# Two transformer blocks on one core: the pace and place of the row fetches beside the router

## The chip, the cores and the metric

One core of a Trainium2 chip runs the whole program. The metric is the device time of one execution in microseconds; the figure of the kernel before is the median of three runs, 1791.49 us (1789.15 to 1792.43). Matrix products run on TensorE (PE, with its weight loads in a row of their own, PEld), elementwise work on VectorE (DVE) and ScalarE (ACT). SyncE (SP) issues the streamed weight loads, GpSimd (POOL) issues the gathers. All DMAs run on the same 16 DMA engines.

## The reference, cut to what matters

Two blocks follow one another on 256 tokens of width 1024, in f32. Each block is a mixer (projections, attention or retention or recurrence, an output projection) and then a PEER layer; the change is in the PEER layers alone:

```
q = (xb @ w_q)                    # 8 heads, 2 halves of 128
s1, s2 = q1 @ k1.T, q2 @ k2.T     # 128 keys a half
top 16 of each half, then the top 16 of their 256 sums -> 16 experts a head, gates g = softmax
h = sum_d u[idx] * x              # u: 16384 x 1024
y = sum_k gelu(h) * g * v[idx]    # v: 16384 x 1024
```

So each token picks 128 of 16384 experts (8 heads of 16), and needs their rows of `u` and of `v`.

## The kernel before, in words

**Two ways to the experts.** `G` = 104 tokens have their rows gathered from HBM, one gather per 128 (token, head, expert) places: 104 row fetches from `u`, then 104 from `v`, each 128 rows of 1024 f32 into one tile `rows`. The other `N` = 152 tokens go through all 16384 experts densely: 128 products with blocks of `u` (`products_of`, L1434), a gate matrix from one-hots (`gate_product`, L1394) and 128 products with blocks of `v` (L1491).

**Stages of one PEER layer, all in the program order of PE.** (1) The queries: 32 units, 16 per tile of 128 tokens (`for t`, `for hc`); each is 8 accumulated products with a 512 KB block of `w_q` (L1322), and the score products of two units earlier (L1311). (2) 128 units of `u`. (3) 128 units of `v`. The weights of all three come as a stream of 512 KB loads (`load_to`, L98) from SP into 4 + 3 buffers; a load goes out as soon as a buffer is used up.

**The router** (`routing`, a generator) runs on DVE beside stages 1 and 2. For tile 0 it takes the heads in order: `route_head` picks the 16 best of either half and of the sums (`best16`, L1194 to L1202), and after every second head `decode` (L1226 to L1249) turns places into expert numbers `eif` (L1272). Then `spread` copies these to the places of the gathers: 12 small products on PE (L1147) that read `eif`, and copies on ACT into `ei` (L1156). From then on `fetch_rows` may issue the gathers of these heads from POOL (L1089). After tile 0 come the eight heads of tile 1, two larger decodes, the softmax, and transposes on PE (L1296). Only when the generator is at its end (`not side`) do the 38 gate blocks (`at`) begin, spread over the remaining units of `u`.

**Who paces what.** After each unit `beside(us, rows)` adds `rows` to a goal and uses gathered rows up to it (`use_rows`; on DVE L1103 for `u`, L1112 for `v`), each use letting `fetch_rows` issue one more gather. Then it lets the router go on by `step(1000.0 * us - 1310.0 * rows, 1)`: the budget is in planned nanoseconds of DVE, and each piece of the router yields its planned cost. In the queries `rows` is 0 for tile 0 and 0.3 a unit for tile 1; in stage 2 it is 0.5 a unit before the first gate block and 0.98 from there; in stage 3 the rest is spread evenly (`pace`). A row has 5 buffers of its own and 3 that are free while whole blocks stream, so up to 8 can be fetched or waiting. The heads known so far bound it too (`fetch["known"]`).

**Scales by column.** `scales_by_column` (L1184, 4 products on PE) and `scaled` (L1190, 4 multiplications on DVE) make `un`, the normalised activations of the dense tokens, which the first unit of stage 2 reads. They stand beside units 8 to 12 of tile 1.

**Order.** Every engine runs its instructions in the order in which the program above emits them; semaphores between engines are put in by the framework.

Of the kernel before, what the change touches and what calls it, by code (L numbers as in the profile page):

```python
# [51 lines left out]
def two_blocks_kernel(ctx: ExitStack, tc: tile.TileContext, a: dict, out: bass.AP, dbg=None, stop=None):  # L52
# [156 lines left out]
    def bank_b(name):  # L209
        return pp_b.tile([P, 512], F32, tag="b", name=name)  # L210
# [788 lines left out]
    def peer(which, norm, names, shared, gelu, after):  # L999
        keys_name, gain_name, u_rows, v_rows = names  # L1000
        with ExitStack() as es:
# [67 lines left out]

            order = [list(col), sorted(col)]  # L1070
            fetch = {"known": 0, "issue": 0, "use": 0, "goal": 0.0}
            fetched, acc, folds = {}, {}, []
            in_rows = [0, 0]

            def fetch_rows():
                while fetch["issue"] < 2 * G:
                    n = fetch["issue"]
                    c, j = divmod(n, G)
                    key = order[c][j]
                    if key[1] >= fetch["known"]:  # L1080
                        return
                    if in_rows[0] < ROW_BUFS[0]:
                        k, t = 0, gp.tile([P, D], F32, tag="rows", name="rows")
                    elif in_rows[1] < ROW_BUFS[1] and n < 2 * G - 8 and units[st["use"] - 1][0] in WHOLE:
                        k, t = 1, spl_p.tile([P, D], F32, tag="lo", name="rows")
                    else:
                        return
                    in_rows[k] += 1
                    nc.gpsimd.indirect_dma_start(  # L1089
                        out=t, out_offset=None, in_=tables[c],  # L1090
                        in_offset=bass.IndirectOffsetOnAxis(ap=ei[:, col[key]:col[key] + 1], axis=0))
                    fetched[n] = k, t, clock[0]
                    fetch["issue"] += 1
# [98 lines left out]
            def best16(v, i, s, w, cost):  # L1192
# [9 lines left out]
                nc.vector.max_index(i[:, 8:16], v[:, 8:16], w)  # L1202
                yield cost

            def route_head(t, h):

                for c in range(2):
                    yield from best16(v_t[:, c, :], i_t[:, h, t, c, :], s_all[:, h, t, c, :], tmp, 320)
                v1, v2 = v_t[:, 0, :], v_t[:, 1, :]
                for o, a0, na, nb in ((0, 0, 1, 16), (16, 1, 3, 8), (40, 4, 4, 4), (56, 8, 8, 1)):  # L1210
                    sh = [P, na, nb]
                    nc.vector.tensor_tensor(
                        cand[:, o:o + na * nb].rearrange("p (a b) -> p a b", a=na),
                        bc(v1[:, a0:a0 + na, None], sh), bc(v2[:, None, 0:nb], sh), op=ALU.add)
                yield 660
                yield from best16(top[:, t, h, :], pos[:, t, h, :], cand, tmp[:, 0:64], 270)
# [46 lines left out]
            def routing():  # L1263

                for h in range(8):
                    while not heads[0]:
                        yield None
                    yield from route_head(0, heads[0].pop(0))
                    if h % 2:
                        yield from decode(0, h - 1, 2)  # L1270
                        hs = slice(h - 1, h + 1)
                        nc.vector.scalar_tensor_tensor(  # L1272
                            eif, fid[:, 0, 0, hs, :].rearrange("p h k -> p (h k)"), 128.0,
                            fid[:, 1, 0, hs, :].rearrange("p h k -> p (h k)"), op0=ALU.mult, op1=ALU.add)
                        w = G // 4
                        spread(eif, 2, ei[:, (h // 2) * w:(h // 2 + 1) * w])
                        fetch["known"] = h + 1
                        fetch_rows()
                exps(0)
                for h in range(8):  # L1280
                    while not heads[1]:
                        yield None
                    yield from route_head(1, heads[1].pop(0))
                    if h == 0:
                        softmax(0)
                        spread(gt[:, 0].rearrange("p h k -> p (h k)"), 8, gg)
                    if h == 3:
                        yield from decode(1, 0, 4)
                exps(1)
                yield from decode(1, 4, 4)  # L1290
                softmax(1)
                pts = [tpp.tile([P, 512], F32, tag="tp", name="pt") for c in range(2)] + [bank_b("pt")]
                for c, pt in enumerate(pts):
                    for t in range(2):
                        v = gt[:, t] if c == 2 else fid[:, c, t]
                        nc.tensor.transpose(pt[:, t * P:(t + 1) * P], v.rearrange("p h k -> p (h k)"), ident)  # L1296
                yield None
                for c, pt in enumerate(pts):
                    nc.scalar.activation(idx[:, c, :], pt[:, G:T], AF.Copy)
                yield None  # L1300
                yield None
# [26 lines left out]
            def beside(us, rows=0.0):  # L1328

                clock[0] += us  # L1330
                fetch["goal"] += rows
                use_rows(int(fetch["goal"]))
                step(1000.0 * us - 1310.0 * rows, 1)

            for t in range(2):
                for hc in range(16):
                    q = query(t, hc)
                    if t == 0 and hc == 0:
                        square_sums(x_ss, 0, (1,))
                        scales(0)  # L1340
                    nc.scalar.activation(qts[hc % 4], q, AF.Copy)
                    if t == 0 and hc == 1:
                        scales_done(0)
                        to_plain(1, range(4, 8), norm)
                        nc.vector.scalar_tensor_tensor(gain, x_sb[:, 0, :], rs[:, 0:1], gain, op0=ALU.mult, op1=ALU.mult)
                        side.append(routing())
                    if hc > 1:
                        score(t, hc - 2)
                    elif t == 1:
                        score(0, hc + 14)  # L1350
                    if t == 0 and hc == 2:
                        square_sums(x_ss, 1, (1,))
                        scales(1)
                    if t == 0 and hc == 3:
                        scales_done(1)
                    if t == 0 and hc == 4:
                        for g in range(ng):
                            own_rows(g)
                    if t == 1 and hc == 8:
                        by_column = scales_by_column()  # L1360
                    if t == 1 and 9 <= hc < 13:
                        scaled(by_column, 2 * (hc - 9))
                    beside(2.05, 0.3 * t)

            sh = [P, 4, P]
            io = bc(iota[:, None, :], sh)
# [71 lines left out]
            for n in range(NE):  # L1438
# [21 lines left out]
                if n >= 2:  # L1460
                    hidden_apply(n - 2)
                hidden(n)
                beside(2.45 if at else 2.07, 0.98 if at else 0.5)
            assert len(at) == NB and at[-1] + 4 < NE
            hidden_apply(NE - 2)
            hidden_apply(NE - 1)
# [263 lines left out]
```

## Time and profile before

| | |
|---|---|
| median of three runs | 1791.49 us |
| the profiled execution's own time | 1787.17 us |
| its span | 1785.1 us |
| PE busy | 1730.7 us, 97% |
| PE weight loads busy | 1617.5 us, 91% |
| DVE / ACT / POOL busy | 64% / 33% / 29% |
| moved by DMA | 590.69 MB, mean 331 GB/s |
| mean granted TensorE clock | 0.994 |
| chain that ended last | PE 75%, DMA 18%, DVE 3%, issue 2% |

The span runs from the first to the last instruction on the chip; 2.07 us of the profiled execution lie around it. Layer 1's PEER part fills about 257 to 931 us of the span, layer 2's about 1094 to 1773 us. A line of the chain of waits names what the last instruction hung on, step by step backwards; a share there is time on that path, while a busy share is not.

### The profile page before, as it was taken

What the parts mean: (1) busy time and instruction counts of PE and PEld (TensorE: products, weight loads), DVE (VectorE), ACT (ScalarE), POOL (GpSimd) and SP (SyncE); (2) the same over time, 40 slices, a digit from 0 to 9 for tenths busy, and PEclk for the clock granted to TensorE, in tenths of its full rate; (3) what the DMA queues carried; (4) which work ended last, traced back from release to release, by engine and by line L of the source; (5) the groups of instructions that cost most, each with busy time, mean ns of one, the idle gap of its engine ahead of it and who ended that gap; (6) DMA issues with size and microseconds to landing.
All of it is one profiled execution on the core that took longest, in us unless ns stands there. A gap on an engine that the chain in (4) does not pass through costs nothing.

```text
span 1785.1 us, 32628 instructions
## 1 busy us (share of the span) xinstructions
PE 1730.7 (97%) x12468; PEld 1617.5 (91%) x12468; DVE 1135.8 (64%) x2694; ACT 597.4 (33%) x1643; POOL 509.5 (29%) x456
## 2 busy tenths in 40 slices
PE   8999998999999999999999998999999999999997
PEld 6878888999999999989988777899999999989997
DVE  5555658797678864444455545789767885444444
ACT  6665542322666520000007564231266660000001
POOL 0000012122344444444411001212234445444440
PEclk9999999999999999999999999999999999999999
DMA  7433569899999999999985226989999999999995
GB/s 267 145 116 132 177 195 343 299 364 393 389 402 418 411 413 419 419 418 419 419 321 197 96 74 217 354 299 380 377 396 416 417 404 419 418 419 419 418 419 218
DMA packets 162219, 590.69 MB, mean 331 GB/s; under 512 B 18272, under 2 KB 18432, under 8 KB 161808
## 3 DMA queue, kind: packets, MB, share of 16 engines
q1 hardware_dynamic: 99648, 362.07, 53.3%
q0 software_dynamic: 62128, 226.22, 32.1%
q8 instruction: 98, 1.61, 0.3%
q14 instruction: 57, 0.47, 0.1%
q10 hardware_dynamic: 288, 0.33, 0.1%
HBM read 585.40 MB, written 1.05 MB: 329 GB/s over the span
## 4 chain that ended last, share of the span: by engine, by line
PE 75%; DMA 18%; DVE 3%; issue 2%; ACT 1%; SPq 0%; ACTq 0%; DVEq 0%
PE h L1434 30%; DMA raw<-in_v_dram 16%; PE y L1491 15%; PE pj L296 5%; PE pj L298 5%; PE q L1322 5%; PE pj L297 5%; PE g L1394 4%; DMA raw<-in_w_q_dram 1%; PE spread L1147 1%; PE sc L476 1%; PE hs L797 1%; PE sps L1311 1%; DMA x_sb<-in_x_dram 0%; PE o L296 0%
## 5 line engine op out<-in xcount | busy, mean ns | idle before, releaser
L1491 PE MATMUL y<-XA,raw 128*128 128x152 f32 x4096 | 556.9, 295 | 14.5 <-DMA raw<-in_v_dram 8.7
L1491 PEld LDWEIGHTS y<-XA,raw 128*128 128x128 f32 x4096 | 534.2, 190 | 39.7 <-DMA raw<-in_v_dram 33.5
L1434 PE MATMUL h<-un,raw 128*128 128x152 f32 x4096 | 544.0, 293 | 0.0
L1434 PEld LDWEIGHTS h<-un,raw 128*128 128x128 f32 x4096 | 533.0, 190 | 0.0
L1089 POOL DMA_INDIRECT rows<-in_u_rows_dram,ei x208 | 223.8, 1076 | 489.1 <-DVE hg L1103 271.5
L1089 POOL DMA_INDIRECT rows<-in_v_rows_dram,ei x208 | 263.6, 1268 | 318.2 <-DVE acc L1112 248.5
L1112 DVE SCALAR_TENSOR_TENSOR acc<-rows,ag,acc 128x1024 f32<-128x1024 f32 x202 | 259.5, 1285 | 2.8
L1103 DVE CUSTOM_DVE_ANT_0 rows<-rows,xg 128x1024 f32<-128x1024 f32 x208 | 253.0, 1218 | 0.0
L116 ACT ACTIVATE hi<-raw 128x1024 fp32r<-128x1024 f32 (+1 forms) x109 | 114.3, 1052 | 339.3 <-DMA raw<-in_w_in_dram 288.4
L1502 DVE MEMSET XA<- 128x1 f32 x128 | 7.6, 59 | 285.7 <-PE y L1491 238.5
L117 DVE TENSOR_TENSOR lo<-raw,hi 128x1024 fp32r<-128x1024 f32 (+1 forms) x109 | 132.5, 1221 | 84.4 <-ACT hi L116 83.7
L1322 PE MATMUL q<-act,raw 128*128 128x128 f32 x1024 | 132.2, 283 | 11.1 <-issue 7.6
L1322 PEld LDWEIGHTS q<-act,raw 128*128 128x128 f32 x1024 | 125.0, 198 | 14.6 <-issue 9.2
L296 PE MATMUL pj<-hi,act 128*128 128x512 f32 x320 | 131.6, 411 | 2.2 <-ACT hi L116 1.3
L298 PE MATMUL pj<-hi,act_l 128*128 128x512 f32 x320 | 125.7, 393 | 0.1
L297 PE MATMUL pj<-lo,act 128*128 128x512 f32 x320 | 125.7, 393 | 0.0
L1422 ACT ACTIVATE XA<-h 128x152 f32<-128x152 f32 (+36 forms) x252 | 65.9, 262 | 159.6 <-PE h L1434 153.0
L1036 POOL DMA_DIRECT2D gain<-in_gain_dram x2 | 1.1, 534 | 398.8 <-PE out L298 252.9
L1520 ACT ACTIVATE XA<-y 128x384 f32<-128x384 f32 (+1 forms) x6 | 2.5, 456 | 290.9 <-DVE XA L1519 290.9
L1399 DVE TENSOR_TENSOR XA<-g,XA 128x216 f32<-128x216 f32 (+18 forms) x76 | 40.6, 535 | 83.5 <-PE g L1394 33.1
L1394 PE MATMUL g<-b,b 128*128 128x128 f32 x608 | 80.1, 275 | 0.0
L1419 ACT ACTIVATE hb<-h 128x4 f32<-128x4 f32 (+36 forms) x148 | 36.8, 249 | 121.1 <-PE h L1434 110.9
(371 smaller groups left out, 1823.3 us busy)
## 6 DMA issues: line engine op xcount, KB each, us to landing
raw<-in_u_dram SPq DMA_DIRECT2D x256, 512.0 KB
raw<-in_v_dram SPq DMA_DIRECT2D x256, 512.0 KB
raw<-in_w_in_dram SPq DMA_DIRECT2D x79, 512.0 KB
raw<-in_w_q_dram SPq DMA_DIRECT2D x64, 512.0 KB
raw<-in_w_out_dram SPq DMA_DIRECT2D x16, 512.0 KB
raw<-in_w_mix_dram SPq DMA_DIRECT2D x12, 512.0 KB
rows<-in_u_rows_dram,ei POOLq DMA_INDIRECT x208
rows<-in_v_rows_dram,ei POOLq DMA_INDIRECT x208
```

Source lines behind the costliest of these rows:

```text
L116: nc.scalar.activation(hi[:, c], src[:, c], AF.Copy)
L117: nc.vector.tensor_tensor(lo[:, c], src[:, c], hi[:, c].bitcast(F32), op=ALU.subtract)
L296: nc.tensor.matmul(ps[t], lhsT=ah, rhs=wh[:, j, :], start=(k == 0), stop=False)
L297: nc.tensor.matmul(ps[t], lhsT=ah, rhs=wl[:, j, :], start=False, stop=False)
L298: nc.tensor.matmul(ps[t], lhsT=al, rhs=wh[:, j, :], start=False, stop=(k == last))
L1089: nc.gpsimd.indirect_dma_start(out=t, out_offset=None, in_=tables[c], in_offset=bass.IndirectOffsetOnAxis(ap=ei[:, col[key]:col[key] + 1], ...
L1103: nc.vector.tensor_tensor_reduce(t, t, xg[:, g, :], 1.0, 0.0, ALU.mult, ALU.add, hg[:, k:k + 1])
L1112: nc.vector.scalar_tensor_tensor(acc[g], t, ag[:, k:k + 1], acc[g], op0=ALU.mult, op1=ALU.add)
L1322: nc.tensor.matmul(q, lhsT=w[:, k * P:(k + 1) * P], rhs=acts["x"][:, k, t * P:(t + 1) * P], start=(k == 0), stop=(k == KT - 1))
L1394: nc.tensor.matmul(gs[k][:, j, :], lhsT=b2[:, j, :], rhs=b1[:, j, :], start=True, stop=True)
L1434: nc.tensor.matmul(hs[n], lhsT=w[:, k * P:(k + 1) * P], rhs=un[:, k, :], start=(k == 0), stop=(k == KT - 1))
L1491: nc.tensor.matmul(block(d), lhsT=w[:, d * P:(d + 1) * P], rhs=XA[:, n, :], start=(n == 0 and d % nb == 0), stop=(n == NE - 1), skip_group ...
```

## The change

Five edits, all in `peer`, so all of them count twice. While the current unit is one of `w_q`, a gather is issued only if fewer than 4 are issued and not yet used. The spread of the expert numbers, with the `known` and `fetch_rows` behind it, and the spread of tile 0's gates, are put off until the next head has emitted the first of its two column searches. The scales by column move from tile 1's units 8 to 12 to tile 0's units 7 to 11. The rates go from 0.3 to 0.4 rows a unit in tile 1's queries and from 0.5 to 0.62 in stage 2 before the first gate block; the planned budget of the router goes from 1000 to 1050 a microsecond. And the generator gives way once more between the last softmax and the transposes.

```diff
-                    if key[1] >= fetch["known"]:
+                    if key[1] >= fetch["known"] or units[st["use"] - 1][0][0] == "w" and n - fetch["use"] >= 4:
                         return
...
+            def known(h):
+                w = G // 4
+                spread(eif, 2, ei[:, (h // 2) * w:(h // 2 + 1) * w])
+                fetch["known"] = h + 1
+                fetch_rows()
...
                 for c in range(2):
+                    while c and pending:
+                        pending.pop(0)()
                     yield from best16(v_t[:, c, :], i_t[:, h, t, c, :], s_all[:, h, t, c, :], tmp, 320)
...
-                        w = G // 4
-                        spread(eif, 2, ei[:, (h // 2) * w:(h // 2 + 1) * w])
-                        fetch["known"] = h + 1
-                        fetch_rows()
+                        pending.append(lambda h=h: known(h))
...
-                        spread(gt[:, 0].rearrange("p h k -> p (h k)"), 8, gg)
+                        pending.append(lambda: spread(gt[:, 0].rearrange("p h k -> p (h k)"), 8, gg))
...
                 softmax(1)
+                yield None
...
-                step(1000.0 * us - 1310.0 * rows, 1)
+                step(1050.0 * us - 1310.0 * rows, 1)
...
-                    if t == 1 and hc == 8:
+                    if t == 0 and hc == 7:
                         by_column = scales_by_column()
-                    if t == 1 and 9 <= hc < 13:
-                        scaled(by_column, 2 * (hc - 9))
-                    beside(2.05, 0.3 * t)
+                    if t == 0 and 8 <= hc < 12:
+                        scaled(by_column, 2 * (hc - 8))
+                    beside(2.05, 0.4 * t)
...
-                beside(2.45 if at else 2.07, 0.98 if at else 0.5)
+                beside(2.45 if at else 2.07, 0.98 if at else 0.62)
```

## Rows read from the trace of the kernel before

**Rows 1.** Windows: length; busy us of PE, PEld, DVE, ACT, POOL; clock, DMA share, GB/s.

```profile
291.50:303.42 11.92, 8.03 (x40) 7.53 (x39) 8.70 (x35) 1.27 (x5) 3.74 (x4) 0.71 1.02 411
303.42:340.90 37.48, 35.75 (x319) 35.56 (x319) 28.52 (x129) 10.85 (x45) 4.06 (x5) 1.00 0.83 277
340.90:443.00 102.10, 102.10 (x796) 102.10 (x796) 92.56 (x349) 25.31 (x77) 27.25 (x26) 1.00 0.98 372
443.00:643.00 200.00, 200.00 (x1593) 200.00 (x1592) 151.08 (x318) 117.25 (x422) 81.36 (x74) 1.00 1.01 405
643.00:931.00 288.00, 281.40 (x2049) 267.19 (x2048) 137.15 (x173) 2.64 (x3) 124.30 (x97) 1.00 1.01 407
...
700.00:720.00 20.00, 19.35 (x142) 18.23 (x141) 8.26 (x12) 0.00 (x0) 8.19 (x7) 1.00 1.03 419
...
1131.44:1142.72 11.28, 7.55 (x40) 6.94 (x39) 8.52 (x33) 1.31 (x5) 3.74 (x4) 0.71 1.02 403
...
1482.60:1773.30 290.70, 282.76 (x2063) 268.97 (x2062) 138.73 (x177) 2.32 (x4) 124.12 (x98) 1.00 0.99 401
```

**Rows 2.** Timeline of PE around 300 us: start, duration, what, idle before.

```profile
291.72 0.97 PE L1322 MATMUL q<-act,raw 128*128 128x128 f32 x5
...
297.20 0.59 PE L1322 MATMUL q<-act,raw 128*128 128x128 f32 x2 [1.72 <-issue]
...
299.58 3.62 PE L1322 MATMUL q<-act,raw 128*128 128x128 f32 x16
...
303.42 1.96 PE L1322 MATMUL q<-act,raw 128*128 128x128 f32 x16
...
305.44 1.95 PE L1322 MATMUL q<-act,raw 128*128 128x128 f32 x16
```

**Rows 3.** Timeline of POOL over the first gathers of layer 1.

```profile
286.43 1.00 POOL L1089 DMA_INDIRECT rows<-in_u_rows_dram,ei  x1 [19.63 <-ACT ei L1156]
...
295.22 0.93 POOL L1089 DMA_INDIRECT rows<-in_u_rows_dram,ei  x1 [0.30 <-issue]
305.38 0.94 POOL L1089 DMA_INDIRECT rows<-in_u_rows_dram,ei  x1 [9.22 <-DVE XA L1200]
```

**Rows 4.** Timeline of DVE in the same stretch.

```profile
295.08 0.18 DVE L1226 TENSOR_SCALAR XA<-XA 128x32 uint32<-128x32 uint32 x1 [0.84 <-DVE XA L1202]
```

**Rows 5.** The page's costliest groups: busy, mean ns, idle before.

```profile
L1491 PEld LDWEIGHTS y<-XA,raw 128*128 128x128 f32 x4096 | 534.2, 190 | 39.7 <-DMA raw<-in_v_dram 33.5
L1434 PE MATMUL h<-un,raw 128*128 128x152 f32 x4096 | 544.0, 293 | 0.0
...
L1103 DVE CUSTOM_DVE_ANT_0 rows<-rows,xg 128x1024 f32<-128x1024 f32 x208 | 253.0, 1218 | 0.0
```

**Rows 6.** Chain of waits, layer 1: the first 17 units of stage 3.

```profile
643.14 35.15 PE y L1491 x272
```

**Rows 7.** Timeline of PE: spreads of layer 1 in the queries, transposes in stage 2.

```profile
284.25 1.51 PE L1147 MATMUL spread<-eif,c_sel 128*128 128x32 f32 x12
...
331.23 1.51 PE L1147 MATMUL spread<-eif,c_sel 128*128 128x32 f32 x12 [1.73 <-DVE eif L1272]
...
443.04 0.60 PE L1296 MATMUL pt<-ident,XA 128*128 128x128 f32 x4
```

**Rows 8.** Timeline of DVE: second head, its decode, expert numbers; next decode's end; softmax.

```profile
272.49 0.29 DVE L1194 MAX8 XA<-XA 128x8 f32<-128x128 f32 x1 [1.17 <-ACT XA L1314]
...
277.46 0.18 DVE L1226 TENSOR_SCALAR XA<-XA 128x32 uint32<-128x32 uint32 x1
...
284.00 0.19 DVE L1272 SCALAR_TENSOR_TENSOR eif<-XA 128x32 f32<-128x32 f32 x1
...
302.92 0.19 DVE L1272 SCALAR_TENSOR_TENSOR eif<-XA 128x32 f32<-128x32 f32 x1
...
435.04 0.29 DVE L1261 TENSOR_TENSOR gt<-gt,XA 128x128 f32<-128x128 f32 x1
```

**Rows 9.** DVE groups of layer 1's queries: the multiplications that make `un`.

```profile
L1190 DVE TENSOR_TENSOR un<-act,rows 128x304 f32<-128x304 f32 x4 | 1.9, 464 | 7.4 <-PE rows L1184 7.4
```

More of the change, by code (lines that the diff above doesn't have):

```diff
@@ L1071, in peer @@
             fetch = {"known": 0, "issue": 0, "use": 0, "goal": 0.0}
-            fetched, acc, folds = {}, {}, []
+            fetched, acc, folds, pending = {}, {}, [], []
             in_rows = [0, 0]
```

## The prediction

> **What bounds the kernel now.** The windows by stage come first, because each stage has its own limit [rows 1]. In stage 2 PE is busy for the whole of both windows (102.10 of 102.10 us, 200.00 of 200.00 us), and the page's group of its products has no idle time before it [rows 5]: PE is the bound there, with DMA at 372 and then 405 GB/s. In stage 3 the link runs at 407 GB/s over 288 us, its tail included (419 inside it), and PE's weight loads stand idle for 39.7 us in the two layers, 33.5 of them ended by a landing block of `v` [rows 5]: there the link is the bound. The chain shows what PE alone would need: the first 17 units, whose blocks had landed ahead, took 35.15 us, 2.068 us a unit [rows 6], so 128 take 264.7 us. Layer 1 used 288.0, layer 2 290.7 [rows 1]. The first ends with the next mixer's loads, the second with its folds; either way some 20 us a layer are lost to bytes.
>
> The queries are odd. PE takes 2.02 us a unit where nothing stops it (303.42 to 305.44) [rows 2]. The two units from 291.50 to 303.42 took 11.92 us [rows 1]. [...] DVE has holes in the same microseconds (0.84 us before L1226) [rows 4]. Just before, from 286.43, POOL issued eight gathers back to back, the eighth at 295.22 [rows 3]. The same stands in layer 2, 11.28 us for two units [rows 1]. I read it as one event: a burst of gathers that holds up every engine, whatever carries it.
>
> **The limit of four.** The stall's price is 11.92 - 2 x 2.02 = 7.88 us and 11.28 - 4.04 = 7.24 us. PE broke off as the fifth of the eight gathers was being issued (one each 1.26 us from 286.43) [rows 2, 3]. With the limit, four go out at the first `known`, and the next only as one is used. Blocks of `w_q` had to share the link with the burst, but PE didn't wait for them, so they lose no cover. I take the stall as gone: -15.1 us in both layers. The bounds: nothing gained, and the whole of it. What is late next: at the first use in stage 2 the limit falls away, three are left and five go out back to back, just where the stall set in. The nearest row is the old burst, in which PE had no gap until the fifth; I take 1 us a layer, between 0 and another 7.9. Net -13.1 us.
>
> [...]
>
> **The rates.** The planner's numbers can be added by hand. Before: 16 x 0.3 + 51 x 0.5 + 77 x 0.98 = 105.8, so 105 rows are used when stage 3 begins. That the first gate block stands at unit 51 follows from the trace too: the transposes at 443.04 [rows 7] come after unit 47 (443.04 - 340.9 us, less two spreads of 1.25 and two score products of 0.2, are 48 units of 2.068), and the generator gives way three more times behind them. After: the router's share of a unit in stage 2 is 1050 x 2.07 - 1310 x 0.62 = 1361 planned ns, where it was 1000 x 2.07 - 1310 x 0.5 = 1415. Some 48 units at 1415 are 67.9 us of plan; less about 1.4 that the wider budgets in the queries do earlier, 66.5 / 1361 is 49 units. With the extra pause the first block comes at 53. Then 16 x 0.4 + 53 x 0.62 + 75 x 0.98 = 112.8: 112 rows, seven more.
>
> A row fetch moves 128 x 1024 f32, 0.524 MB, as a unit does. At the 419 GB/s that stage 3 carries while PE waits for it [rows 1] it takes 1.251 us. Before, stage 3 uses 103 rows beside 128 blocks: 231 x 1.251 / 128 is 2.26 us a unit against PE's 2.068; after, with 96 rows, 2.19 us. The link stays the bound, so seven fetches are worth 7 x 1.251 = 8.76 us a layer, -17.5 us. The bounds: nothing, if PE begins to wait in stage 2 instead, and 8.76. For that I weigh the load there: 1.62 x 0.524 / 2.068 is 411 GB/s before the first gate block, where 372 passed in the trace, and from the first block on it stays near the 405 of before [rows 1]. Both lie under 419, the first by 2%, and it begins with the five fetches at once. I take the full gain less 1 us a layer for waits of PE: -15.5 us.
>
> **Spreads and scales.** In the queries PE waited 1.73 us for `eif` at the third spread and hardly at the first [rows 7]; layer 2 shows the same pair. The wait at the third goes: its spread comes a unit later. The first gets worse. The four multiplications cost DVE 464 ns each [rows 9], and three now lie ahead of the first `eif`; DVE was already the one that PE met there (284.00 + 0.19 against 284.25) [rows 7, 8]. Since the first column search fits into the same unit's budget, the spread isn't put off past a product: +1.4 us. Queued behind that waiting spread on PE are the next unit's products, and behind `ei` the gathers.
>
> Then DVE has no stall to catch up in. A head takes it 277.46 - 272.49 = 4.97 us for 5.21 planned, a decode with its `eif` 284.19 - 277.46 = 6.73 for 5.0 [rows 8]: two heads and a decode are 16.7 for 15.4. From the first to the second `eif` it needs some 17 us (302.92 - 284.00, less 2.5 for five holes, the longest of which stands in [rows 4], plus the fourth multiplication), PE about 17.3: no wait. For the third, 16.7 and five rows at 1.22 us [rows 5] are 22.8, PE's ten units and a spread 21.5, 1.3 us short with 0.3 of margin left from the second; the fourth is alike, with a little less. I take 1.2 us for these together, with 0 and 3 as bounds. 1.4 + 1.2 - 1.73 is +0.85 us a layer, +1.7. The transposes hold: DVE's softmax was done at 435.33, PE came at 443.04 [rows 7, 8], 7.7 us, and PE comes 4 us later now. `scales_by_column` itself is four products of PE, moved and not added. On ACT and SP nothing moves but the copies behind the spreads.
>
> **The sum.** -13.1 - 15.5 + 1.7 = -26.9 us. The profiled execution took 1787.17 us (span 1785.1), so 1760.3; the median of the timed runs lies 4.3 above the profiled one, so I predict 1764.6 us.
>
> **The rivals.**
> 1. *The stall stays, or comes in stage 2 instead.* For it: five gathers still go out together there, and PE broke off at the fifth. Against it: three fewer follow. Then only the rows' gain is left: 1791.5 - 15.5 + 1.7 = 1777.7 us.
> 2. *The link takes the gain back.* Stage 2 at 411 GB/s finds the link full, PE waits there for `u`, and stage 3 begins with less landed. For it: 411 is all that the stall's window moved, with work queued throughout. Against it: 405 passed for 200 us with PE never waiting. Then the stall's gain is left: 1791.5 - 13.1 + 1.7 = 1780.1 us.
> 3. *Slower: any burst of four or more stalls.* Then there are two a layer, at the first `known` and at the start of stage 2, each with its stretch at the lower clock. The old stall's 7.6 us and the 7.76 - 0.85 = 6.9 that rows and spreads leave make 14.5, so it turns slower once a burst costs more than 7.25 us. At 12, the eight-gather stall and half again, it is 24 - 14.5 = 9.5 us a layer, 1810.5 us. Against it: PE ran through the first four without a gap [rows 2, 3].
> 4. *Only recorded executions stall.* Then timed runs have nothing of it to lose, and again 1777.7 us. For it: the holes of PE and DVE come together and have no semaphore. [...]
> 5. *It does little:* the bursts never form or the rows land as before, 1791 us.
>
> **How the numbers follow.** Forecast 0.60 (own range 1754 to 1773), rival 1 0.14, rival 2 0.11, rival 3 0.06, rival 4 0.05, rival 5 0.04. A measurement here can tell about 0.2%, 3.6 us, from no change. Faster: the forecast and rivals 1, 2 and 4, 0.60 + 0.14 + 0.11 + 0.05 = 0.90, less 0.04 for cases that meet: 0.86. Slower: rival 3 and a piece of these, 0.07. Same: 0.07. The range takes in rivals 1, 2 and 4, both bounds of the burst and of the link, and leaves out rivals 3 and 5 and the tails: 1753 to 1782 us.
>
> **What would show it.** Right: no gap inside a query unit and a clock of 1.00 in both layers; at most four gathers back to back there; queries of about 76 us, where 257.64 to 340.90 are 83.3 now; 96 gathers used in stage 3 and 8 to 9 us less in each. Wrong: a stretch of "issue" gaps at the first units of `u`, idle time before L1434, or stage 3 as long as now. The first spread should wait 1 to 2 us for `eif`, the third not at all.

## The result, and the profile after

The changed kernel took 1758.96 us (median of 4 runs, 1755.73 to 1760.83), the kernel before 1790.88 beside it (4 runs, 1789.15 to 1792.43): a ratio of 0.982, 95% interval 0.980 to 0.984. The forecast was 1764.6. The profiled execution took 1755.73 us with a span of 1754.0, 31.1 us under that of before, where the sum said 26.9.

The windows of the changed kernel, stage 2 ahead of the transposes, stage 2 from there, stage 3 of layer 1 and 20 us within it (length; busy us of PE, PEld, DVE, ACT, POOL; clock, DMA share, GB/s), answer to [rows 1]:

```profile
332.40:441.00 108.60, 108.60 (x848) 108.60 (x847) 100.16 (x364) 26.34 (x80) 37.45 (x36) 1.00 1.02 413
441.00:635.00 194.00, 194.00 (x1545) 194.00 (x1544) 148.91 (x305) 116.32 (x418) 81.94 (x72) 1.00 1.02 407
635.00:918.00 283.00, 277.60 (x2059) 267.81 (x2057) 130.96 (x169) 3.57 (x4) 112.85 (x91) 1.00 1.00 404
700.00:720.00 20.00, 20.00 (x156) 19.92 (x155) 9.95 (x13) 0.00 (x0) 7.95 (x7) 1.00 1.03 419
```

PE is still busy for the whole of stage 2, though 413 GB/s pass where 372 did. Stage 3 is 7 us shorter in layer 1. The page's groups (answer to [rows 5]) say by what: idle time ahead of `v`'s weight loads is 26.0 us for both layers and was 39.7.

```profile
L1499 PEld LDWEIGHTS y<-XA,raw 128*128 128x128 f32 x4096 | 532.9, 190 | 26.0 <-DMA raw<-in_v_dram 20.2
...
L1442 PE MATMUL h<-un,raw 128*128 128x152 f32 x4096 | 544.0, 293 | 0.0
```

PE's timeline in layer 1's queries (answer to [rows 2, 7]): the first spread now waits 1.40 us for `eif`. Of the long stall one broken unit is left. Its two gaps of 0.34 and 0.44 us are put down to "issue", that is, to no semaphore that the profile shows, and the next unit begins 3.20 us after it began, where an unbroken one takes 2.01. Layer 2 has such a unit too, of 3.15 us. The clock stayed at 1.00 in both (290 to 298, 1114 to 1122).

```profile
284.84 1.50 PE L1148 MATMUL spread<-eif,c_sel 128*128 128x32 f32 x12 [1.40 <-DVE eif L1282]
...
292.31 0.84 PE L1330 MATMUL q<-act,raw 128*128 128x128 f32 x6
...
293.49 0.27 PE L1330 MATMUL q<-act,raw 128*128 128x128 f32 x1 [0.34 <-issue]
...
294.20 1.26 PE L1330 MATMUL q<-act,raw 128*128 128x128 f32 x9 [0.44 <-issue]
...
295.51 1.95 PE L1330 MATMUL q<-act,raw 128*128 128x128 f32 x16
```

POOL (answer to [rows 3]) issued five gathers back to back, at 287.02, 288.32, 289.59, 290.83 and 292.07, not four. The sixth waited for DVE, which frees a row buffer when it has used the first row.

```profile
287.02 1.00 POOL L1090 DMA_INDIRECT rows<-in_u_rows_dram,ei  x1 [21.02 <-ACT ei L1157]
...
292.07 0.94 POOL L1090 DMA_INDIRECT rows<-in_u_rows_dram,ei  x1 [0.30 <-issue]
303.59 0.94 POOL L1090 DMA_INDIRECT rows<-in_u_rows_dram,ei  x1 [10.58 <-DVE XA L1199]
```

The length of each stage, from PE's first product in it to its first in the next, in the two profiled executions (layer 1 / layer 2, us):

| stage | before | after | difference, both | by the prediction |
|---|---|---|---|---|
| ahead of the queries | 257.6 / 161.3 | 256.8 / 160.2 | -1.9 | 0 |
| queries | 83.1 / 85.9 | 75.5 / 79.3 | -14.2 | -15.1 + 1.7 |
| stage 2 | 302.3 / 302.3 | 302.3 / 302.3 | 0.0 | +2 burst, +2 waits |
| stage 3 | 290.0 / 290.8 | 283.0 / 282.9 | -14.9 | -17.5 |
| sum | | | -31.0 | -26.9 |

### The profile page after: what moved, and what is told of

It is laid out like the page before. It is cut to its first block, busy times and chain, and to the rows that moved or that the text cites. A ratio compares the mean times of both kernels' runs of the same rounds, so it can differ in the third digit from the quotient of the medians.

```text
span 1754.0 us, 32614 instructions
## 1 busy us (share of the span) xinstructions
PE 1716.0 (98%) x12468; PEld 1611.6 (92%) x12468; DVE 1131.4 (65%) x2690; ACT 596.7 (34%) x1639; POOL 506.8 (29%) x456
## 5 line engine op out<-in xcount | busy, mean ns | idle before, releaser
L1499 PE MATMUL y<-XA,raw 128*128 128x152 f32 x4096 | 547.7, 294 | 8.8 <-DMA raw<-in_v_dram 5.2
L1090 POOL DMA_INDIRECT rows<-in_v_rows_dram,ei x208 | 257.4, 1238 | 351.7 <-DVE acc L1113 283.0
L1330 PE MATMUL q<-act,raw 128*128 128x128 f32 x1024 | 127.4, 278 | 3.7 <-DMA raw<-in_w_q_dram 2.2
L1330 PEld LDWEIGHTS q<-act,raw 128*128 128x128 f32 x1024 | 121.0, 194 | 6.4 <-issue 3.1
L1430 ACT ACTIVATE XA<-h 128x152 f32<-128x152 f32 (+35 forms) x252 | 66.3, 263 | 164.9 <-PE h L1442 140.5
L1528 ACT ACTIVATE XA<-y 128x384 f32<-128x384 f32 (+1 forms) x6 | 2.5, 457 | 282.9 <-DVE XA L1527 282.9
L1407 DVE TENSOR_TENSOR XA<-g,XA 128x224 f32<-128x224 f32 (+18 forms) x76 | 40.9, 538 | 71.9 <-PE g L1402 28.2
L1402 PEld LDWEIGHTS g<-b,b 128*128 128x128 f32 x608 | 75.2, 192 | 0.0
(371 smaller groups left out, 1780.7 us busy)
```

What stands on the lines that cost most here:

```text
L1090: nc.gpsimd.indirect_dma_start(out=t, out_offset=None, in_=tables[c], in_offset=bass.IndirectOffsetOnAxis(ap=ei[:, col[key]:col[key] + 1], ...
L1330: nc.tensor.matmul(q, lhsT=w[:, k * P:(k + 1) * P], rhs=acts["x"][:, k, t * P:(t + 1) * P], start=(k == 0), stop=(k == KT - 1))
L1402: nc.tensor.matmul(gs[k][:, j, :], lhsT=b2[:, j, :], rhs=b1[:, j, :], start=True, stop=True)
L1499: nc.tensor.matmul(block(d), lhsT=w[:, d * P:(d + 1) * P], rhs=XA[:, n, :], start=(n == 0 and d % nb == 0), stop=(n == NE - 1), skip_group ...
```

## The experiments

They ran in four sets, each on one chip with the kernel before beside it; the sets turned out to differ, so each says how long the kernel before took.

### Set 1 (before: 1790.43 us, 7 runs): one part alone

limit_alone is the kernel before with the limit and nothing else:

```diff
-                    if key[1] >= fetch["known"]:
+                    if key[1] >= fetch["known"] or units[st["use"] - 1][0][0] == "w" and n - fetch["use"] >= 4:
```

> The kernel before with the limit of four as its only edit. Theory A (the stall in the queries is the price of the eight gathers at once, and it is there in timed runs too): the two broken units of 11.92 and 11.28 us shrink to about 5.1 each (one gap of 1.1 us is left, as in the changed kernel), stage 3 stays at 288 to 291 us a layer, and the time falls by about 13 us to 1778. Rival (only recorded executions stall): the trace shows the same mend, but the time stays within 4 us of 1791. Rival (the link takes it back): stage 3 grows by what the queries lose, 1791.

rates_alone is the kernel before with the rates and the budget alone:

```diff
-                step(1000.0 * us - 1310.0 * rows, 1)
+                step(1050.0 * us - 1310.0 * rows, 1)
-                    beside(2.05, 0.3 * t)
+                    beside(2.05, 0.4 * t)
-                beside(2.45 if at else 2.07, 0.98 if at else 0.5)
+                beside(2.45 if at else 2.07, 0.98 if at else 0.62)
```

> The kernel before with 0.4 and 0.62 rows a unit and the budget of 1050, and nothing else. Theory A (each row moved ahead of stage 3 is worth its 1.25 us of link): seven rows fewer in stage 3, which falls by 7 to 9 us a layer, the stall in the queries stays at 7 to 8 us a layer, the time falls by about 15 us to 1776. Rival (the router pays: with 1050 and more rows DVE comes late and PE waits at the spreads and transposes): stage 2 grows beyond 302.3 us and the gain is under 8 us.

Measured: limit_alone 1777.87 us, ratio 0.994 (0.992 to 0.996); rates_alone 1771.15 us, ratio 0.989 (0.988 to 0.991). That is -12.6 and -19.3, together -31.8, and the whole change gave -31.9. limit_alone, of which 13 us were expected, worked in its own stage: it shortened the queries to 76.7 / 82.7 us and left stage 3 at 289.8 / 289.5 (in layer 2 the first spread waited 2.25 us, before 0.21, which takes part of the gain back). rates_alone kept the stall (PE's gaps with no semaphore in the queries add up to 4.1 and 3.7 us, before to 3.9 and 3.7) and cut stage 3 to 284.2 / 281.4, with 88 fetches left for it. It gained 4 us more than the 15 expected, and it reached the other stages too: the third spread no longer waited in the queries, and stage 2 took 304.9 / 303.2 us where it had taken 302.3, after a wait of the fourth spread in each layer. The page's group of `v`'s weight loads in limit_alone, then in rates_alone, shows the same split:

```profile
L1491 PEld LDWEIGHTS y<-XA,raw 128*128 128x128 f32 x4096 | 534.0, 190 | 38.4 <-DMA raw<-in_v_dram 32.8
```

```profile
L1491 PEld LDWEIGHTS y<-XA,raw 128*128 128x128 f32 x4096 | 532.8, 190 | 25.9 <-DMA raw<-in_v_dram 19.1
```

In PE's timeline of rates_alone the third spread of layer 1 doesn't wait, though no spread is put off in that kernel; the fourth, in stage 2, does:

```profile
328.56 1.50 PE L1147 MATMUL spread<-eif,c_sel 128*128 128x32 f32 x12
...
351.73 1.50 PE L1147 MATMUL spread<-eif,c_sel 128*128 128x32 f32 x12 [0.67 <-DVE eif L1272]
```

### Set 1: the size and the place of the burst

limit_three is the changed kernel with `>= 3` for `>= 4`, burst_in_stage2 with `>= 0`, so that the program emits no gather before stage 2.

> The changed kernel with a limit of three instead of four. In the changed kernel five gathers went out back to back, since the fifth waits for no buffer on the chip, and one gap of 1.1 us followed in each layer. Theory A (the number of gathers not yet landed sets the stall): with four back to back the gap is gone, 2.2 us less, 1757. Rival (the link carrying gathers alone sets it): the gap stays at about 1 us, for the link still carries gathers alone for some 2 us; the time is that of the changed kernel, 1759.

> The changed kernel with a limit of none in the queries, so that the first gathers go out eight at once behind the fourth spread, in unit 6 of stage 2, while a block of u is fetched every 2.07 us. Theory A (number of gathers not yet landed): PE breaks off inside products of u without a semaphore, for some 4 to 8 us, near the sixth gather. Rival (the link carrying gathers alone): no such gap, stage 2 as long as before but for waits that name eif, gt or a landing block. The time is worth little here: the queries use no rows, so DVE catches up in stage 2 and the last products may wait for it.

Measured: limit_three 1760.47 us, ratio 0.984 (0.982 to 0.985), as the change itself. burst_in_stage2 1782.94 us, one run, with its stall in the queries (PE's gaps with no semaphore add up to 2.6 and 3.7 us) and a stage 2 of 306.8 / 308.6 us, where the changed kernel took 302.3. Neither did what its text assumes. POOL's timeline of limit_three begins with five gathers, again 1.25 us apart:

```profile
288.32 1.00 POOL L1090 DMA_INDIRECT rows<-in_u_rows_dram,ei  x1 [20.28 <-ACT ei L1157]
...
293.39 0.93 POOL L1090 DMA_INDIRECT rows<-in_u_rows_dram,ei  x1 [0.30 <-issue]
304.87 0.93 POOL L1090 DMA_INDIRECT rows<-in_u_rows_dram,ei  x1 [10.55 <-DVE XA L1199]
```

POOL's of burst_in_stage2 begins with eight, 43 to 52 us before the stage to which the program had put them (stage 2 begins at 340.2):

```profile
288.39 1.00 POOL L1090 DMA_INDIRECT rows<-in_u_rows_dram,ei  x1 [20.25 <-ACT ei L1157]
...
297.19 0.93 POOL L1090 DMA_INDIRECT rows<-in_u_rows_dram,ei  x1 [0.30 <-issue]
344.31 1.68 POOL L1090 DMA_INDIRECT rows<-in_u_rows_dram,ei  x1 [46.19 <-DVE hg L1104]
```

The limit counts in the order in which the program is written. On the chip these timelines show nothing that ties a gather to a unit of PE: POOL went on, with 0.30 us between gathers, until it waited for DVE, which frees the row buffers (10.55 us behind the five, 46.19 behind the eight). What the limit does is to emit these gathers while only the 5 buffers of their own are allowed. Emitted in stage 2 they have 8.

ACT shows what a burst does to the others. Its copy of a query unit follows PE's last product by 0.10 us where nothing holds it (before_again: the unit at 288.88 ended at 290.83, its copy began at 290.93); a copy that comes microseconds later is called held here. This is ACT's timeline of the kernel before, and then of the changed one, around the unit that PE ended at 289.65 and at 290.24 ("remote": the profile can't name what ended the wait):

```profile
287.74 0.28 ACT L1341 ACTIVATE XA<-q 128x128 f32<-128x128 f32 x1
298.00 0.51 ACT L1341 ACTIVATE XA<-q 128x128 f32<-128x128 f32 x2 [9.62 <-remote]
```

```profile
288.32 0.28 ACT L1349 ACTIVATE XA<-q 128x128 f32<-128x128 f32 x1
294.32 0.46 ACT L1349 ACTIVATE XA<-q 128x128 f32<-128x128 f32 x2 [5.36 <-remote]
```

In layer 1 the copy came 8.35 us late with eight gathers and 4.09 with five (2.47 in limit_three, 5.98 in burst_in_stage2), each time 1.1 to 1.9 us after POOL's last gather had ended. In layer 2 the five held it for 4.13 and 2.48 us, the eight for 4.09 and 6.25; with eight it came there while the burst still ran, and the copy of the next unit was held until 2.0 to 2.1 us after the burst. PE ran on meanwhile and broke off only at the longer holds: not at all in limit_three, for under a microsecond a layer in the changed kernel, for 2.6 to 3.9 us in the two with eight. That gave theory A: gathers that POOL issues back to back hold the semaphores of the other engines. Rival B: eight fetches under way do it, however they are issued.

### Set 2 (before: 1780.85 us, 17 runs): spaced gathers, and the small edits

paced_eight is the kernel before with at most one gather a query unit, each behind a small copy on POOL that has to wait for that unit's copy on ACT:

```diff
-                    if key[1] >= fetch["known"]:
+                    paced = units[st["use"] - 1][0][0] == "w"
+                    if key[1] >= fetch["known"] or paced and last[0] == st["use"]:
...
+                    if paced:
+                        last[0] = st["use"]
+                        nc.gpsimd.tensor_copy(tick[:, 0:1], qts[turn_of[0]][:, 0:1])
```

> The kernel before, with one thing changed: in the query stage at most one row gather goes out per query unit, and each stands behind a one-column copy on POOL that reads that unit's query block, so POOL has to wait for ACT's copy of each unit. Up to eight rows are still fetched ahead; there is no limit of four. Theory A (gathers that POOL issues back to back hold the semaphores of the other engines until about 1.5 us after the last one): with gathers 2.1 us apart nothing is held for long, the break in TensorE's queries (7.2 to 7.9 us a layer with the dip of the clock in the kernel before) goes, the query stage takes about 77 us in layer 1 as in limit_alone or less, and the time is about 1777 us. Rival B (what breaks the queries is eight row fetches under way, however they are issued): the break of 7 us a layer stays, at the sixth to eighth gather, and the time is 1788 to 1792 us.

spreads_back and scales_later are the changed kernel with one edit each:

```diff
-                        pending.append(lambda h=h: known(h))
+                        known(h)
```

```diff
-                    if t == 0 and 8 <= hc < 12:
-                        scaled(by_column, 2 * (hc - 8))
+                    if t == 0 and 11 <= hc < 15:
+                        scaled(by_column, 2 * (hc - 11))
```

(spreads_back has the gates' spread issued at once as well.)

> The changed kernel, with the spreads put back behind the head whose ids they carry (they are no longer put off into the next head). By the prediction's step the third spread waits about 1.7 us for DVE again in each layer and the time goes to about 1762 us. The rival: the DVE budget of 1050 ns a us removed that wait (in rates_alone it was gone without the put-off spreads, and the fourth waited 0.9 us): the third waits 0 us, the fourth about 0.9 us, and the time is 1759 to 1761 us.

> The changed kernel, with the row scales by column three query units later (units 11 to 14 of tile 0 and not 8 to 11), so that DVE comes to the first head's ids before it multiplies them. If the first spread waits because DVE does the scales ahead of it, its wait falls from 1.5 us to about 0.2 us in each layer, the query stage is 1.3 us shorter and the time is about 1756 us. The rival: the scales take DVE's time elsewhere and another spread waits instead; the time stays at 1759 us.

Measured: paced_eight 1779.95 us, ratio 1.000 (0.998 to 1.002), with no held copy and no gap. That decides between neither theory: the stall had gone, as A has it, but the kernel before, which keeps its burst of eight, was as fast beside it, 10 us faster than in set 1. All kernels of the set with five gathers back to back had ACT's copies at 0.10 us too. So the stall of the kernel before was itself in question.

spreads_back took 1763.67 us, ratio 0.992 (0.989 to 0.995). In its timeline of PE the third and fourth spreads do not wait, so the prediction's step fell: putting the spreads off isn't what removed that wait. As in rates_alone, the rates and the budget had; that it was the wider budget, and not the rows, is argued (rows only add to DVE's work, 1.22 us each in [rows 5]), not shown.

```profile
323.52 1.40 PE L1148 MATMUL spread<-eif,c_sel 128*128 128x32 f32 x12
...
345.75 1.40 PE L1148 MATMUL spread<-eif,c_sel 128*128 128x32 f32 x12
```

Its time is 5.7 us above that of the changed kernel in set 3, and the intervals of the two ratios overlap; whether putting off the spreads gains anything is left open.

scales_later took 1757.27 us, ratio 0.988 (0.984 to 0.991). Its first spread waits 0.43 us (0.76 in layer 2), where the changed kernel showed 1.40 and 1.32 at first, and in set 3 0.97 and 0.58:

```profile
286.15 1.50 PE L1148 MATMUL spread<-eif,c_sel 128*128 128x32 f32 x12 [0.43 <-DVE eif L1282]
```

In layer 1 this fits the other kernels: the first spread waits 0.65 to 1.40 us in the five profiles with the scales at units 8 to 11, and less than 0.6 in the nine with them elsewhere. In layer 2 it doesn't: it waits 0.58 to 2.57 us with them there and up to 2.26 without (2.25 in limit_alone). So the scales were part of that wait in layer 1 at most, and the 0.7 us by which this kernel's median lies under the changed kernel's in set 3 can't be told from nothing.

### Set 3 (before: 1778.43 us, 13 runs): the same kernels once more

before_again, after_again and paced_again are the kernel before, the changed one and paced_eight, with no edit.

> The kernel before, unchanged, profiled beside paced_again and after_again on one chip. In the second set of runs the kernel before took 1780.85 us (median of 17) where it took 1790.43 us in the first, and the kernels with five gathers back to back (scales_later, spreads_back, best) showed no held copy of ACT (0.10 us behind TensorE), where the same burst held it for 2.5 to 4.1 us in the first set. Theory C (the hold, and the stall with it, depends on the chip or its state and not on the kernel alone): if the kernel before takes about 1781 us again, its profile shows eight gathers back to back with ACT's copies at 0.10 us and no gap of TensorE without a semaphore in the queries; if it takes about 1790 us, the copies are held for 6 to 8 us and the gaps are there. Rival: the stall is there at 1781 us too (7 us a layer), and the 10 us lie elsewhere.

> The changed kernel, unchanged, beside the same runs of the kernel before. By theory C, where the kernel before takes about 1781 us the limit of four has nothing to take away, the changed kernel takes about 1760 us (first spread wait 1.5 us a layer, stage 3 283 us a layer as before) and the ratio is 0.988 to 0.991; where the kernel before takes about 1790 us the ratio is 0.982 again. Rival (the stall is in both sets): the ratio is 0.982 at either time.

> The kernel before with one gather per query unit, each behind a one-column copy on POOL, as in paced_eight. Theory A with C: where the kernel before takes about 1790 us, this one shows no held copy and no gap and takes about 1779 us (ratio 0.994); where the kernel before takes about 1781 us, there is no hold to take away and the two are alike (ratio 1.0). Rival B (eight under way, however issued, break the queries where the chip does it at all): ratio 1.0 at either time.

Measured: before_again 1782.75 us (one run), after_again 1758.01 us, ratio 0.989 (0.985 to 0.992), paced_again 1780.33 us, ratio 1.001 (0.999 to 1.003). Theory C (the hold depends on the chip or its state and not on the kernel alone) held in this one profile. POOL's timeline of before_again has the eight gathers of [rows 3], from 287.62 to 296.40 with the same spaces,

```profile
287.62 1.00 POOL L1089 DMA_INDIRECT rows<-in_u_rows_dram,ei  x1 [19.63 <-ACT ei L1156]
...
296.40 0.94 POOL L1089 DMA_INDIRECT rows<-in_u_rows_dram,ei  x1 [0.30 <-issue]
```

and in the same microseconds ACT's copies come every 2.01 us, with nothing held:

```profile
290.93 0.28 ACT L1341 ACTIVATE XA<-q 128x128 f32<-128x128 f32 x1 [1.37 <-PE q L1322]
292.94 0.28 ACT L1341 ACTIVATE XA<-q 128x128 f32<-128x128 f32 x1 [1.73 <-PE q L1322]
```

The same program stalls in some sets and not in others, and sets 1 to 3 ran on the same chip. From set 1 to set 3 the kernel before became 12 us faster; the changed one took 1758.01 us in set 3, and 1758.96 beside a kernel before of 1790.88.

Without the stall the change still gained 20.4 us of median. The spans of set 3's two profiled executions differ by 22.9 us: stage 3 by 6.8 and 8.8, the queries by 3.2 and 4.9. The latter hold the third spread's wait and what can follow it, a stretch at a lower clock. PE's timeline of before_again, and then of paced_again, which has the same wait:

```profile
324.73 1.84 PE L1147 MATMUL spread<-eif,c_sel 128*128 128x32 f32 x12 [1.73 <-DVE eif L1272]
326.42 3.76 PE L1322 MATMUL q<-act,raw 128*128 128x128 f32 x16
```

```profile
324.26 1.51 PE L1152 MATMUL spread<-eif,c_sel 128*128 128x32 f32 x12 [1.73 <-DVE eif L1277]
325.62 2.03 PE L1327 MATMUL q<-act,raw 128*128 128x128 f32 x16
```

In the first the next unit took 3.76 us, in the second 2.03. The windows of before_again give the clock there, 0.53:

```profile
326.00:333.00 7.00, 7.00 (x36) 7.00 (x37) 6.62 (x35) 1.96 (x11) 0.94 (x1) 0.53 0.55 181
```

The changed kernel isn't free of it: in after_again the first spread's wait of 0.97 us was followed by such a stretch, a unit of 3.38 us and a clock of 0.72 over 6 us, where the wait of 1.40 us in the first profile was followed by units at full pace. So some microseconds of a single profile's time are the clock's (1.7 in that unit of before_again alone, 3.76 us for 2.03), and the spans of before_again and paced_again, 1780.7 and 1771.8 us, differ though their medians' ratio is 1.

```profile
286.38 1.50 PE L1148 MATMUL spread<-eif,c_sel 128*128 128x32 f32 x12 [0.97 <-DVE eif L1282]
287.74 3.38 PE L1330 MATMUL q<-act,raw 128*128 128x128 f32 x16
```

### A faster version, and a test of A against B (sets 2 and 4)

best is the changed kernel with `>= 3`, scales_later, 0.5 rows a unit in tile 1's queries and 1.02 behind the first gate block. best_paced has the pacing of paced_eight for the limit, and 1.08 for 1.02:

```diff
-                    beside(2.05, 0.4 * t)
+                    beside(2.05, 0.5 * t)
...
-                beside(2.45 if at else 2.07, 0.98 if at else 0.62)
+                beside(2.45 if at else 2.07, 1.02 if at else 0.62)
```

> The changed kernel with a limit of three for four, the row scales as in scales_later, 0.5 rows a unit in tile 1's queries for 0.4, and 1.02 rows a unit behind the first gate block for 0.98: five more rows of each layer's 201 are used ahead of stage 3. By the term of the rates that held (1.25 us a row) stage 3 shrinks by 6.3 us a layer, the first spread by 1.3 us, together about 1743 us. The rival: the link has to give about 421 GB/s in the gate blocks where it gave 402 to 417 before, PE waits there for weights or rows by 3 to 6 us a layer, and the time is 1752 to 1758 us.

> The kernel of the run best, with the limit of three replaced by the pacing of paced_eight (one gather per query unit, behind POOL's one-column copy, up to eight fetched ahead), and 1.08 rows a unit behind the first gate block for 1.02: some four more rows of each layer are used ahead of stage 3. By the term of the rates stage 3 shrinks by 4 x 1.25 = 5 us a layer against best and the time is about 1738 us. Rival: the link has to give about 424 GB/s in the gate blocks (414 in best), TensorE waits there and in stage 2 for what stage 3 gives back, and the time is 1746 to 1752 us. If the kernel before takes about 1790 us this time (the state with the hold), theory A says that ACT's copies in the queries stay 0.10 us behind TensorE, rival B that they are held as in the kernel before.

Measured: best 1748.52 us in set 2, ratio 0.984 (0.981 to 0.986). best_paced 1747.98 us in set 4, ratio 0.977 (0.976 to 0.979); the kernel before took 1790.71 us there, as in set 1. best lies between the 1743 us expected and the 1752 to 1758 of its rival; best_paced came out where its rival has it, 1746 to 1752, and not at 1738. POOL's timeline of best_paced begins with nine gathers, 1.6 to 2.7 us apart, each behind its small copy:

```profile
286.00 1.01 POOL L1094 DMA_INDIRECT rows<-in_u_rows_dram,ei  x1 [2.06 <-ACT ei L1161]
287.71 0.18 POOL L1093 COPY pad<-XA 128x1 f32<-128x1 f32 x1 [0.71 <-ACT XA L1353]
288.42 0.99 POOL L1094 DMA_INDIRECT rows<-in_u_rows_dram,ei  x1 [0.52 <-issue]
...
302.65 0.96 POOL L1094 DMA_INDIRECT rows<-in_u_rows_dram,ei  x1 [0.16 <-issue]
```

ACT's timeline has every copy in its place, none later than 0.10 us in either layer:

```profile
289.31 0.28 ACT L1353 ACTIVATE XA<-q 128x128 f32<-128x128 f32 x1 [1.37 <-PE q L1334]
291.32 0.28 ACT L1353 ACTIVATE XA<-q 128x128 f32<-128x128 f32 x1 [1.73 <-PE q L1334]
```

This is theory A's answer, in a set in which the kernel before was as slow as with its stall. The reserves: it is one profile, set 4 ran on another chip than sets 1 to 3, and it has no profile of the kernel before, so that this chip holds copies beside a burst is taken from that time alone. Nine gathers over 17 us, where eight took 9, probably have fewer fetches under way at once too (an estimate, not counted), so B isn't ruled out; what the profile shows is that these nine held nothing.

A trace of set 1, in which copies were held, shows spaced gathers too. In stage 2 of burst_in_stage2 the four gathers from 344.31 took nearly 2 us each, so that POOL issued them 2.0 to 2.3 us apart, and the copies of the four units of `u` that PE ended between 347 and 353.3 came 0.04 us behind their products; layer 2 has the same. Here too fewer gathers were issued in the same time, so it fits A and doesn't exclude B. Its POOL, then its ACT:

```profile
348.59 1.98 POOL L1090 DMA_INDIRECT rows<-in_u_rows_dram,ei  x1 [0.30 <-issue]
350.88 1.99 POOL L1090 DMA_INDIRECT rows<-in_u_rows_dram,ei  x1 [0.30 <-issue]
```

```profile
349.13 0.30 ACT L1430 ACTIVATE XA<-h 128x152 f32<-128x152 f32 x1 [1.77 <-PE h L1442]
351.20 0.30 ACT L1430 ACTIVATE XA<-h 128x152 f32<-128x152 f32 x1 [1.77 <-PE h L1442]
```

The rates went on paying in best: 85 rows left for stage 3 (89 in the changed kernel), which takes 277.5 / 278.2 us, 5.5 and 4.7 less. They stopped in best_paced: 80 and 81 rows, 278.0 / 278.5 us. The windows of stage 3's first 168 us and the next 84, of best and then of best_paced, show where PE waits:

```profile
633.40:801.40 168.00, 166.63 (x1254) 162.55 (x1254) 76.01 (x99) 1.58 (x2) 70.96 (x60) 1.00 1.03 418
801.40:885.40 84.00, 83.38 (x634) 81.81 (x633) 36.81 (x49) 0.00 (x0) 30.67 (x26) 1.00 1.03 418
```

```profile
633.70:801.70 168.00, 165.48 (x1234) 160.12 (x1233) 72.16 (x96) 1.58 (x2) 64.34 (x54) 1.00 1.03 418
801.70:885.70 84.00, 84.00 (x649) 83.74 (x648) 35.18 (x49) 0.00 (x0) 29.18 (x26) 1.00 1.02 414
```

In best_paced PE no longer waits in the later part (84.00 of 84.00 us busy), and the link carries 414 there: that part is PE's, and a row less in it buys nothing any more. But the first part waits longer than in best, 7.9 us of PEld's for 5.5, with the link at 418 in both. Why it does with fewer rows isn't shown; the rival's reading is that stage 2, whose gate blocks had the link at 417 GB/s from 440 to 633 (414 in best), leaves less landed.

## Why the prediction was right, step by step

**The stall.** Its price was a little high: 15.1 us forecast, 12.8 in the profiled executions, since the broken unit that is left still costs 1.2 and 1.1 us. In timed runs limit_alone gave 12.6. That it wasn't a missing block is read from the gaps of the unit that began at 291.72 in the kernel before: 0.98, 1.03 and 1.72 us, each put down to "issue" and none to a landing block, with a clock of 0.82 from 291.5 to 299.5 and of 0.51 in the 4 us behind. Its mechanism was half right. A burst of gathers did hold ACT's copies in set 1 (by 2.47 to 8.35 us in layer 1), where the hold was there at all, but "four go out at the first `known`" was wrong: five did, since the limit acts on the order of emission, and on the chip the first wait was for a row buffer (10.58 us). With it fell two of the signs named, no gap inside a query unit and at most four gathers back to back. And the stall is no property of the kernel alone: in set 3 there was none to take away, and the ratio was 0.989. That the result fell beside a kernel before that took 1790.88 us, as it does with the stall, is luck.

**The burst in stage 2.** +1 us a layer was put at the start of stage 2. Five gathers did go out there, and they held ACT: the copy of the last scores came 1.4 us behind its product, which PE ended at 337.1, and 2.3 us in layer 2 (0.04 in after_again). But PE had no gap (302.3 us before and after). PE's timeline, then ACT's:

```profile
336.72 0.38 PE L1319 MATMUL sps<-XA 128*128 128x128 f32 x2
```

```profile
338.54 0.47 ACT L1322 ACTIVATE XA<-sps,rs 128x256 f32<-128x256 f32 x1 [3.61 <-PE sps L1319]
```

What is left of the stall is in the queries, at the burst of five.

**The rates.** Seven fetches fewer in stage 3 was exact (96 to 89 issued there; the 103 and 96 of the sum are the rows used), the transposes' two units and the first gate block at unit 53 too. Each was worth 1.00 us in layer 1 and 1.13 in layer 2, in set 3 0.97 and 1.26, so 1.09 on average and not 1.251; stage 3 lost 7.0 and 7.9 us where the signs named 8 to 9. That PE's own time takes over in pieces of the stage is argued from windows like the 20 us at 700, where PE is busy for 20.00 us and was for 19.35. The 1 us a layer kept back for waits in stage 2 wasn't needed, at 413 GB/s where 411 was worked out. The two errors nearly met, which is luck: -15.5 forecast, -14.9 measured.

**Spreads and scales.** +1.7 us was forecast, and -1.0 came. The first spread's wait grew by 1.4 and 1.1 us in that profile, about as forecast, and the third's, 1.73 us a layer, went. The 1.2 us for the later ones did not come. The fourth spread waited 0.67 us a layer in rates_alone and not in spreads_back, which has the scales in tile 0 besides; that their move away from it took this wait was not tested by itself. The cause given for the third, a spread that comes a unit later, isn't the one that the runs show: rates_alone and spreads_back lost the wait without it. In the queries this error and that of the stall nearly met as well: -13.4 forecast for both, -14.2 measured.

**The rest.** 1.9 us of the gain lie ahead of the queries, where nothing was changed; that is put down to the scatter of two executions (the four timed runs of either kernel lie 3.3 and 5.1 us apart). The time came out 5.6 us under the forecast because the 4 us kept back in stage 2 weren't needed and these 1.9 came on top, while stage 3 gave 2.6 less; the queries and the distance of the profiled execution from the median (3.2 us, 4.3 before) make about 1 each.

**The rivals.** 1 fell with the shorter queries and stage 2 at 302.3 us, 2 with stage 2 and the shorter stage 3. 3 fell with the bursts in stage 2, which didn't stop PE. 4 can't be decided in the form that it had: limit_alone gained 12.6 us in timed runs, but every run here leaves a span and a clock, so none is known to be without records. A recorded execution need not stall: the recording of the same 32628 instructions did not bring the hold in set 3 (before_again, ACT's copies every 2.01 us). Whether recording has a part in the hold of the other sets was not shown. The rival's argument from DVE was misread: [rows 4] puts DVE's 0.84 us down to DVE's own L1202, so only PE's gaps are without a semaphore.

## What to carry to other kernels

A limit that the program keeps while it emits instructions is no limit on the chip (five gathers went out at a limit of four, eight at one of none): ask which semaphore the queue really meets, and if it meets none, give it one, as the one-column copy did (gathers 1.6 to 2.7 us apart). In stage 3, which the link bounded at 419 GB/s, each transfer moved to a stage where PE had the last word bought about its transfer time (1.0 to 1.3 us for 1.25), and nothing once PE never waited in the part that it was taken from (best_paced: four to five rows fewer than best, 278.0 / 278.5 us for 277.5 / 278.2). Measure a change beside the kernel before every time: over a third of what this one gained (about 12 of 32 us) was a stall that the same program did not have in another set of runs.

## What the runs showed of the hardware that was not expected

Eight gathers issued by POOL at 1.25 us each put off ACT's next copy by 4.1 to 8.4 us behind the product that it waits for, five by 2.5 to 4.1, in sets in which the kernel before took 1790 us; the same gathers held nothing in a profile of set 3, in which it took 1778. What differs between the sets isn't known; sets of both kinds ran on one chip. Spaced 1.6 to 2.7 us apart, nine gathers held nothing in set 4, on another chip.

A wait of PE in the queries can be followed by a stretch at a lower clock or not. The third spread waited 1.73 us in both layers of before_again and of the kernel before: in the first the next units took 3.76 and 3.51 us, with a clock of 0.53 over the 7 us in layer 1, in the second 2.03 in either layer, at 1.00; in paced_again it was 2.03 too, at 1.00 from 323 to 333. Shorter waits of the first spread were followed by slow units as well: 0.97 us in after_again by one of 3.38 (0.72 over 6 us), 0.70 in layer 2 of before_again by one of 3.55.
